# Two mixture-of-experts blocks: wide and narrow expert units alternate, and block 2 fetches tokens in fp32 from x less its mean

## The chip, the cores and the metric

The kernel runs on one core of a Trainium2 chip. The time is that of one execution on the device in microseconds (us), the median of three runs. TensorE is PE in the rows (its weight loads PEld), VectorE is DVE, ScalarE is ACT, GpSimd is POOL, SyncE is SP. All loads of weights are issued by SP on one DMA queue.

## The reference

Two transformer blocks of different make, each of two layers, on 256 tokens of 1024 channels. Each layer is a token mixer and then a mixture of 32 experts. For this text only the experts matter; block 1 has hidden width 512 and an RMS norm ahead, block 2 has hidden width 256 and a layer norm ahead.

```python
def hier_moe(h, ...):                       # block 1; block 2's _hier_moe is alike
    g_sel = argmax(h @ wg + bg)             # one of 4 groups of 8 experts
    top_l, top_i = top_k(e_logits[g_sel], 2)  # two experts of that group
    gates = softmax prob of the group * softmax(top_l)
    ...
    hid = silu(xi @ w1[e]) * (xi @ w3[e])   # for the tokens xi of expert e
    y[tokens of e] += (hid @ w2[e]) * gate
```

All weights are fp32. The routing depends on the data: how many tokens an expert gets is known only when the layer's logits are.

## The kernel before

The program runs four stages of experts, one per layer (block 1's first and second layer, then block 2's), with a mixer ahead of each. An expert stage is one call of `moe`. It works through 11 *units* one after the other. A wide unit has 2 experts with room for 64 tokens each, a narrow unit 4 experts with room for 32, so either fills 128 rows. Per unit PE does this: *fetch* (L878: the selected tokens are gathered by a product of x with a 0/1 matrix `P`, eight slices of 128 channels, then scaled and shifted into `xg`), the first products (L1018: `xg` times w1 and w3, streamed as `w<-A`), and, one unit later, the second products (L932: the hidden values `ht` times w2, streamed as `w<-B`) and the combination (L945). The fetch of the next unit lies between the products of the present one.

The order of units was the same in both blocks: five wide, five narrow, one wide. `PLACES` held (fixed, wide) for each block. The first `fixed` places (4 in block 1, 6 in block 2) are experts by number, whose weights can be asked for in advance. All later places are filled by rank: the class `Ranks` counts the tokens of each late expert, sends those with over 32 to wide places, and gives the order as the tile `kidx`. That comes from a DVE tile `kperm`, a PE product (L724) and a DVE copy (L726). SP reads `kidx` at L753 into registers that address the loads, and can issue no load of a ranked expert before that.

The weight stream goes through a ring of slots of 1 MB: 13 and `EXTRA` more during an expert stage (9 in block 1, 5 in block 2). A load waits at L170 until the last reader of its slot is done. A wide unit in block 1 takes 8 slots of w1 and w3 and 4 of w2, a narrow one twice that; in block 2 half of these. Before `kidx` SP can issue 20 slots in block 1 and 16 in block 2. At the ninth unit after the first (`turn`) stands a branch for experts with over 64 tokens, `overfull` (L767), not taken here; SP waits there until all its loads have landed.

In block 2 the fetch is done with rounded parts: DVE normalises x (L841), ACT rounds it to `xh` (L842), DVE forms the rest `xl` (L851), and the fetch multiplies both by `P` in fp32r, for pairs of units of one kind at a time (256 columns; the first unit and the last narrow and wide ones have 128). In block 1 the fetch is one fp32 product of x itself, and `P` holds the token's norm factor in place of 1. The head of the expert stage (`Head.finish`, L593 to L613) makes the norm's factor and the logits; then the router makes `ras` (chosen experts), `rpos` (the token's place) and `P`.

Of the kernel before, what the change touches and what calls it, by code (L numbers as in the profile page):

```python
# [28 lines left out]
E = 32  # L29
# [22 lines left out]
class Core:  # L52
# [25 lines left out]
    def constants(self, ctx):  # L78
# [31 lines left out]
        self.tok = cp.tile([128, 2, 3], F32, name="tok")  # L110
# [423 lines left out]
class Head:  # L534
# [57 lines left out]
    def finish(self, t):  # L592
# [4 lines left out]
        if self.centred:  # L597
            mv = p.tile([128, 2], F32, name=f"hmv{t}")
            nc.vector.bn_aggr(mv, self.st[:, t])
            nc.vector.tensor_copy(c.tok[:, t, 1:2], mv[:, 0:1])  # L600
            nc.scalar.activation(l[:, 0:1], mv[:, 1:2], AF.Ln, bias=c.col(self.eps))
        else:
            nc.vector.tensor_scalar(l[:, 1:2], self.st[:, t, 0:1], 1.0 / D, self.eps, op0=ALU.mult, op1=ALU.add)
            nc.scalar.activation(l[:, 0:1], self.st[:, t, 1:2], AF.Ln, scale=1.0 / D, bias=l[:, 1:2])
# [6 lines left out]
        else:  # L611
            nc.scalar.activation(c.tok[:, t, 2:3], l[:, 0:1], AF.Exp, scale=0.5)
# [71 lines left out]
class Ranks:  # L684
# [4 lines left out]
    def __init__(self, c, p, ps, as_, fixed, wide):  # L689
# [122 lines left out]
def moe(c, ctx, index, scale, shift, w13, w2, nf, spare, centred, residual, end):  # L812
# [5 lines left out]
    fixed, wide = PLACES[centred]  # L818
# [3 lines left out]
    if centred:  # L822
        groups, k = [units[:1]], 1
        while k < len(units):
            m = 2 if k + 1 < len(units) and units[k + 1][2] == units[k][2] else 1
            groups.append(units[k:k + m])
            k += m
    else:
        groups = [[u] for u in units]
    most = max(map(len, groups)) * 128  # L830
# [6 lines left out]
    if centred:  # L837
# [5 lines left out]
    else:  # L843
        src = (x,)
    pos, as_, rest, chosen = router(c, p, mp, c.L)
    if centred:
        with tc.issue_after(chosen.ins):
            for t in range(2):
                for i in range(2):
                    d = slice(i * 512, i * 512 + 512)  # L850
# [3 lines left out]
    def group(us, first):  # L854

        e0, _, cap = us[0]
        n = sum(u[1] for u in us)
        m = n * cap
        P = p.tile([128, 2, most], F32R if centred else F32, name="P", bufs=2)
        P4 = P[:, :, :m].rearrange("p t (g s) -> p t g s", s=cap)  # L860
        xg = p.tile([128, 8, most], F32, name="xg", tag="xg", bufs=2)

        def select():
            at = pos if e0 < fixed else places["pos"]
            for t in range(2):
                if centred:
                    selected = nc.vector.tensor_tensor(P4[:, t], c.iota[:, None, :cap].to_broadcast([128, n, cap]),
                                                       at[:, t, e0:e0 + n, None].to_broadcast([128, n, cap]),
                                                       ALU.is_equal)
                else:  # L870
                    for i in range(n):
                        selected = nc.vector.tensor_scalar(P4[:, t, i], c.iota[:, :cap], at[:, t, e0 + i:e0 + i + 1],
                                                           c.tok[:, t, 0:1], op0=ALU.is_equal, op1=ALU.mult)
            return selected

        def products(q, k, i, start, stop):
            for t in range(2):
                nc.tensor.matmul(q, src[i][:, t, k * 128:(k + 1) * 128], P[:, t, :m],  # L878
                                 start=start and t == 0, stop=stop and t == 1, skip_group_check=True)

        def modulate(q, k, vector):
            o = xg[:, k, :m]
# [5 lines left out]
        def fetch(k):  # L888
            def f():
                q = mp.tile([128, 512], F32, name="ms")[:, :m]  # L890
                for i in range(len(src)):
                    products(q, k, i, i == 0, i == len(src) - 1)
# [3 lines left out]
        def fetch_all():  # L896
            qs = [yp.tile([128, 512], F32, name="y", tag="y", bufs=4) for _ in range(4)]
            for i in range(len(src)):
                for k in range(8):
                    q = qs[k % 4][:, (k // 4) * m:(k // 4 + 1) * m]  # L900
                    products(q, k, i, i == 0 and k < 4, i == len(src) - 1)
                    if i == len(src) - 1:
                        modulate(q, k, k % 2)
        return P4, xg, [select] + ([fetch_all] if first else [fetch(k) for k in range(8)])

    P, xg, steps = group(groups[0], True)
# [3 lines left out]
    with tc.issue_after(selected.ins):  # L910
        ranks = Ranks(c, p, mp, as_, fixed, wide)
        places["pos"] = ranks.ordered(pos, "kpos")
        w, cnt = rest(ranks.excess)
    wp = w
    if not centred:

        wp = p.tile([128, 2, 32], F32, name="rwp")
        nc.vector.tensor_mul(wp, w, c.tok[:, :, 2:3].to_broadcast([128, 2, 32]))
# [30 lines left out]
    def back(pr, j):  # L949
# [3 lines left out]
        nc.vector.tensor_mul(Pw.rearrange("p t (g s) -> p t g s", s=cap), P[:, :, j:j + ne, :].bitcast(F32),  # L953
# [22 lines left out]
    for g, us in enumerate(groups):  # L976
        if g:
            P, xg = nxt[:2]
        nxt = group(groups[g + 1], False) if g + 1 < len(groups) else (None, None, [])
        share = -(-len(nxt[2]) // len(us))  # L980
        for unit in us:
            e0, ne, cap = unit
            j = e0 - us[0][0]
            n = units.index(unit)
            last = n == len(units) - 1
            todo = [nxt[2].pop(0) for _ in range(min(share, len(nxt[2])))]
            pr = {"n": n, "unit": unit, "h": []}
            who = experts(unit)
            begun = None
            if n == turn - 1:  # L990

                keep = c.hold(extra)
                held = None if centred else c.hold(extra)
                out, gate = residual(mp, keep, c.scratch(), held)
            if n == turn:
                begun = first(who, 0)
                room, hT = [c.scratch(), c.scratch()], c.scratch()
                hT = hT.rearrange("p (a b) -> p a b", b=256)
                count = nc.values_load(cnt[0:1, 0:1], min_val=0, max_val=E * CAP,
                                       skip_runtime_bounds_check_because="counts of tokens")  # L1000
                overfull(c, sp, None if centred else c.tok, scale, shift, out, w, pos, count, nf, *spare, gate, room,
                         hT, ranks)
                c.loaded = None
# [1267 lines left out]
```

## Time and profile before

| | |
|---|---|
| median of three runs | 2426.05 us (2425.70 to 2428.39) |
| the profiled execution | 2428.38 us, span 2426.6 us |
| PE busy | 2149.3 us, 89% of the span |
| DVE, ACT busy | 885.9 us (37%), 751.9 us (31%) |
| DMA queue of the weight loads | 772.85 MB, 79.7% of the 16 engines' span |
| TensorE clock, mean granted | 0.955 |
| expert stages, roughly | 293 to 768, 919 to 1395, 1650 to 1897, 2165 to 2412 us |

Shares are averages over unlike stages; in the expert stages both PE and the DMA engines are near full, and which of them waits changes with the kind of unit.

### The profile page before, as it was taken

What the parts mean: (1) busy time and instruction counts of PE and PEld (TensorE: products, weight loads), DVE (VectorE), ACT (ScalarE), POOL (GpSimd) and SP (SyncE); (2) the same over time, 40 slices, a digit from 0 to 9 for tenths busy, and PEclk for the clock granted to TensorE, in tenths of its full rate; (3) what the DMA queues carried; (4) which work ended last, traced back from release to release, by engine and by line L of the source; (5) the groups of instructions that cost most, each with busy time, mean ns of one, the idle gap of its engine ahead of it and who ended that gap; (6) DMA issues with size and microseconds to landing.
All of it is one profiled execution on the core that took longest, in us unless ns stands there. A gap on an engine that the chain in (4) does not pass through costs nothing. (4 is left out here: it accounts for less than half of the span.)

```text
span 2426.6 us, 32734 instructions
## 1 busy us (share of the span) xinstructions
PE 2149.3 (89%) x12546; PEld 1230.8 (51%) x12546; DVE 885.9 (37%) x1983; ACT 751.9 (31%) x1493; POOL 44.9 (2%) x48
## 2 busy tenths in 40 slices
PE   7999899987678989999767799998998899999977
PEld 4667633322225864333222287994432678974422
DVE  3864511110013762111000354973121647861112
ACT  3642312211004442222111244562211445642212
POOL 0001000000000200000000000000000000000000
PEclk8999999999999998999999899998999989989998
DMA  9977499999999356999999961556999923549997
GB/s 393 403 271 306 174 397 401 417 421 421 386 421 389 119 217 274 400 418 421 421 420 389 421 243 48 197 195 236 377 413 370 381 92 139 191 157 360 409 393 277
DMA packets 119846, 775.13 MB, mean 319 GB/s; under 512 B 14185, under 2 KB 15593, under 8 KB 35450
## 3 DMA queue, kind: packets, MB, share of 16 engines
q1 hardware_dynamic: 119674, 772.85, 79.7%
q8 instruction: 106, 1.74, 0.3%
q14 instruction: 66, 0.54, 0.1%
HBM read 771.75 MB, written 1.05 MB: 318 GB/s over the span
## 5 line engine op out<-in xcount | busy, mean ns | idle before, releaser
L1018 PE MATMUL s<-w,xg 128*32 128x512 f32 (+1 forms) x3072 | 606.9, 617 | 67.9 <-DMA w<-A 59.8
L932 PE MATMUL s<-w,ht 128*32 128x512 f32 (+1 forms) x1536 | 348.4, 617 | 44.8 <-DMA w<-B 43.0
L1018 PEld LDWEIGHTS s<-w,xg 128*32 128x32 f32 (+1 forms) x3072 | 141.8, 121 | 369.2 <-issue 216.5
L396 PE MATMUL pj<-hi,wh 128*128 128x256 f32 x864 | 243.8, 285 | 3.4 <-ACT sg L1800 2.4
L397 PE MATMUL pj<-lo,wh 128*128 128x256 f32 x864 | 243.3, 283 | 0.0
L398 PE MATMUL pj<-hi,wl 128*128 128x256 f32 x864 | 240.4, 284 | 0.0
L935 DVE SCALAR_TENSOR_TENSOR yl<-s,ws,yh 128x512 fp32r<-128x512 f32 x88 | 66.0, 750 | 357.5 <-ACT yh L934 354.5
L932 PEld LDWEIGHTS s<-w,ht 128*32 128x32 f32 (+1 forms) x1536 | 82.6, 122 | 224.5 <-issue 138.5
L391 ACT ACTIVATE wh<-w 128x512 fp32r<-128x512 f32 x248 | 154.4, 631 | 120.0 <-PE pj L397 89.5
L1022 DVE TENSOR_TENSOR hid<-hid,s 128x256 f32<-128x256 f32 x66 | 27.7, 419 | 439.4 <-ACT hid L1021 439.3
L392 DVE TENSOR_TENSOR wl<-w,wh 128x512 fp32r<-128x512 f32 x248 | 167.2, 689 | 50.3 <-ACT wh L391 45.7
L396 PEld LDWEIGHTS pj<-hi,wh 128*128 128x128 f32 x864 | 166.1, 193 | 9.7 <-ACT sg L1800 2.8
L398 PEld LDWEIGHTS pj<-hi,wl 128*128 128x128 f32 x864 | 164.4, 192 | 4.8 <-issue 2.1
L397 PEld LDWEIGHTS pj<-lo,wh 128*128 128x128 f32 x864 | 166.3, 192 | 0.1
L934 ACT ACTIVATE yh<-s,ws 128x512 fp32r<-128x512 f32 x88 | 60.5, 688 | 323.0 <-PE s L932 290.6
L359 DVE TENSOR_TENSOR wl<-w,wh 128x512 fp32r<-128x512 f32 (+2 forms) x164 | 112.6, 695 | 100.1 <-ACT wh L358 83.9
L1021 ACT ACTIVATE hid<-s 128x256 f32<-128x256 f32 x66 | 25.3, 384 | 394.3 <-PE s L1018 394.1
L886 ACT ACTIVATE xg<-ms,mod,gain 128x128 f32<-128x128 f32 x160 | 72.8, 457 | 204.8 <-PE ms L878 202.4
L358 ACT ACTIVATE wh<-w 128x512 fp32r<-128x512 f32 (+2 forms) x164 | 99.6, 614 | 114.5 <-PE pj L344 56.1
L878 PEld LDWEIGHTS ms<-P,x 128*128 128x128 f32 x640 | 85.3, 197 | 66.5 <-issue 35.8
L344 PE MATMUL pj<-wl,hi 128*128 128x512 f32 (+2 forms) x272 | 107.1, 395 | 0.0
L878 PE MATMUL ms<-P,x 128*128 128x128 f32 x640 | 103.7, 294 | 2.0 <-issue 1.6
(638 smaller groups left out, 2731.2 us busy)
## 6 DMA issues: line engine op xcount, KB each, us to landing
w<-A SPq DMA_DIRECT2D x384, 1024.0 KB, 12.1
w<-B SPq DMA_DIRECT2D x128, 1024.0 KB, 17.9
w<-B SPq DMA_DIRECT2D x128, 512.0 KB, 10.2
w<-ada SPq DMA_DIRECT2D x48, 1024.0 KB, 9.8
w<-wi SPq DMA_DIRECT2D x48, 1024.0 KB, 9.4
w<-w SPq DMA_DIRECT2D x26, 1024.0 KB, 15.6
w<-wo SPq DMA_DIRECT2D x16, 1024.0 KB, 5.8
w<-wbr SPq DMA_DIRECT2D x8, 1024.0 KB, 4.8
```

Source lines behind the costliest of these rows:

```text
L344: nc.tensor.matmul(qs[t][:, :n], a, wl[:, :n], start=False, stop=False)
L358: nc.scalar.activation(wh[:, :n], w[:, k], AF.Copy)
L359: nc.vector.tensor_sub(wl[:, :n], w[:, k], wh[:, :n].bitcast(F32))
L391: nc.scalar.activation(wh, w[:, k], AF.Copy)
L392: nc.vector.tensor_sub(wl, w[:, k], wh.bitcast(F32))
L396: nc.tensor.matmul(d, wh[:, e], hi, start=k == 0 and ch % 2 == 0, stop=False, skip_group_check=True)
L397: nc.tensor.matmul(d, wh[:, e], lo, start=False, stop=False, skip_group_check=True)
L398: nc.tensor.matmul(d, wl[:, e], hi, start=False, stop=k == nk - 1, skip_group_check=True)
L878: nc.tensor.matmul(q, src[i][:, t, k * 128:(k + 1) * 128], P[:, t, :m], start=start and t == 0, stop=stop and t == 1, skip_group_check=True)
L886: nc.scalar.activation(o, q, AF.Identity, bias=shift[:, k:k + 1], scale=scale[:, k:k + 1])
L932: nc.tensor.matmul(q[cap * i:cap * i + cap, :], ht[:, o * cap:o * cap + cap], pr["w2"][i][:, half, f * 512:f * 512 + 512], start=f == 0, s ...
L1018: nc.tensor.matmul(q[cap * i:cap * i + cap, :], xg[:, k, e * cap:(e + 1) * cap], ws[m][:, k, 512 * o:512 * o + 512], start=k == 0, stop=k ...
```

## The change

Four parts. `PLACES` now holds the order of units as a string: in block 1 w w n w n w n w n n w, in block 2 w w w n w n w n n n w; the numbers of wide and narrow units stay, and so do the three units at the branch. `Ranks` gets the list `at`, which says which rank stands at which place. In block 2 the normalisation on DVE and the parts `xh` and `xl` go; instead ACT takes the mean from x in place (L612, in the head), `P` holds the norm factor as in block 1, the token weights are multiplied by its inverse, and the fetch is the fp32 product of block 1, unit by unit. `EXTRA` is 9 in both blocks.

```diff
@@ Head.finish
         if self.centred:
             mv = p.tile([128, 2], F32, name=f"hmv{t}")
             nc.vector.bn_aggr(mv, self.st[:, t])
-            nc.vector.tensor_copy(c.tok[:, t, 1:2], mv[:, 0:1])
+            nc.vector.tensor_scalar(c.tok[:, t, 1:2], mv[:, 0:1], -1.0, None, op0=ALU.mult)
...
-        else:
-            nc.scalar.activation(c.tok[:, t, 2:3], l[:, 0:1], AF.Exp, scale=0.5)
+
+            nc.scalar.activation(c.x[:, t], c.x[:, t], AF.Identity, bias=c.tok[:, t, 1:2])
+        nc.scalar.activation(c.tok[:, t, 2:3], l[:, 0:1], AF.Exp, scale=0.5)
@@ Ranks.__init__
-        nc.vector.tensor_copy(row[:, 0:wide - 2], c.places[:, 0:wide - 2])
-        nc.vector.tensor_copy(row[:, wide - 2:E - 2], c.places[:, wide:E])
-        nc.vector.tensor_copy(row[:, E - 2:E], c.places[:, wide - 2:wide])
+        i = 0
+        while i < E:
+            n = 1
+            while i + n < E and at[i + n] == at[i] + n:
+                n += 1
+            nc.vector.tensor_copy(row[:, i:i + n], c.places[:, at[i]:at[i] + n])
+            i += n
@@ moe
-    units = [(n, 2, CAP) for n in range(0, wide - 2, 2)] + [(n, 4, CAP // 2) for n in range(wide - 2, E - 2, 4)]
-    units.append((E - 2, 2, CAP))
...
+    units, at = [], []
+    wide = 2 * form.count("w")
+    nextw, nextn = 0, wide
+    for f in form:
+        n = 2 if f == "w" else 4
+        units.append((len(at), n, 128 // n))
+        if f == "w":
+            at, nextw = at + list(range(nextw, nextw + n)), nextw + n
+        else:
+            at, nextn = at + list(range(nextn, nextn + n)), nextn + n
...
-        src = [p.tile([128, 2, 1024], F32R, name=n) for n in ("xh", "xl")]
-        for t in range(2):
-            nc.vector.tensor_scalar(x[:, t], x[:, t], c.tok[:, t, 1:2], c.tok[:, t, 0:1], op0=ALU.subtract, op1=ALU.mult)
-            nc.scalar.activation(src[0][:, t], x[:, t], AF.Copy)
...
-                    nc.vector.tensor_sub(src[1][:, t, d], x[:, t, d], src[0][:, t, d].bitcast(F32))
...
-        def products(q, k, i, start, stop):
+        def products(q, k, start):
             for t in range(2):
-                nc.tensor.matmul(q, src[i][:, t, k * 128:(k + 1) * 128], P[:, t, :m],
-                                 start=start and t == 0, stop=stop and t == 1, skip_group_check=True)
+                nc.tensor.matmul(q, x[:, t, k * 128:(k + 1) * 128], P[:, t], start=start and t == 0, stop=t == 1,
+                                 skip_group_check=True)
...
-EXTRA = (9, 5)
-PLACES = ((4, 12), (6, 12))
+EXTRA = (9, 9)
+PLACES = ((4, "wwnwnwnwnnw"), (6, "wwwnwnwnnnw"))
```

How it moves instructions shows on PE between the first fetch product of an expert stage and the product that yields `kidx`. This is PE in block 2's first layer before, from behind the first 24 fetch products (rounded parts `xh` and `xl`) on; `s` is the bank of the first unit's first products, `kperm,places` the product that gives `kidx`. The second layer reads the same.

```order
L709 MATMUL ms<-kover,kafter 32x1
L710 MATMUL ms<-kover,lt 32x1
L711 MATMUL ms<-ones,kover 128x1
L878 MATMUL y<-P,xl 128x128 x2
L1018 MATMUL s_12376<-w,xg 64x512 x2
L878 MATMUL y<-P,xl 128x128 x2
L1018 MATMUL s_12376<-w,xg 64x512 x2
L878 MATMUL y<-P,xl 128x128 x2
L1018 MATMUL s_12376<-w,xg 64x512 x2
L878 MATMUL y<-P,xl 128x128 x2
L1018 MATMUL s_12376<-w,xg 64x512 x3
L724 MATMUL ms<-kperm,places 1x32
```

After the change the same place reads thus, behind eight fp32 fetch products of x; each of these is two instructions in a trace.

```order
L714 MATMUL ms<-kover,kafter 32x1
L715 MATMUL ms<-kover,lt 32x1
L716 MATMUL ms<-ones,kover 128x1
L861 MATMUL y<-P,x 128x128 x2
L992 MATMUL s_12386<-w,xg 64x512 x2
L861 MATMUL y<-P,x 128x128 x2
L992 MATMUL s_12386<-w,xg 64x512 x2
L861 MATMUL y<-P,x 128x128 x2
L992 MATMUL s_12386<-w,xg 64x512
L861 MATMUL y<-P,x 128x128 x2
L992 MATMUL s_12386<-w,xg 64x512 x4
L729 MATMUL ms<-kperm,places 1x32
```

The number of first products ahead of `kidx` is nine in both; the fetch products are 16 in place of 32. In block 2's second layer the scheduler now puts only five ahead:

```order
L861 MATMUL y<-P,x 128x128 x8
L714 MATMUL ms<-kover,kafter 32x1
L715 MATMUL ms<-kover,lt 32x1
L716 MATMUL ms<-ones,kover 128x1
L861 MATMUL y<-P,x 128x128 x2
L992 MATMUL s_17185<-w,xg 64x512 x2
L861 MATMUL y<-P,x 128x128 x2
L992 MATMUL s_17185<-w,xg 64x512 x2
L861 MATMUL y<-P,x 128x128 x4
L992 MATMUL s_17185<-w,xg 64x512
L729 MATMUL ms<-kperm,places 1x32
```

There `kidx` has moved ahead of four first products. In block 1 it moves the other way. This is PE in block 1's second layer before, the same place:

```order
L878 MATMUL y<-P,x 128x128 x8
L709 MATMUL ms<-kover,kafter 32x1
L710 MATMUL ms<-kover,lt 32x1
L711 MATMUL ms<-ones,kover 128x1
L878 MATMUL y<-P,x 128x128 x2
L1018 MATMUL s_6750<-w,xg 64x512 x2
L878 MATMUL y<-P,x 128x128 x2
L1018 MATMUL s_6750<-w,xg 64x512 x2
L878 MATMUL y<-P,x 128x128 x4
L1018 MATMUL s_6750<-w,xg 64x512
L724 MATMUL ms<-kperm,places 1x32
```

And now:

```order
L861 MATMUL y<-P,x 128x128 x8
L714 MATMUL ms<-kover,kafter 32x1
L715 MATMUL ms<-kover,lt 32x1
L716 MATMUL ms<-ones,kover 128x1
L861 MATMUL y<-P,x 128x128 x4
L992 MATMUL s_6762<-w,xg 64x512 x4
L861 MATMUL y<-P,x 128x128 x2
L992 MATMUL s_6762<-w,xg 64x512 x2
L861 MATMUL y<-P,x 128x128 x2
L992 MATMUL s_6762<-w,xg 64x512 x3
L729 MATMUL ms<-kperm,places 1x32
```

Nine first products stand ahead of `kidx` where five stood (in the first layer seven where five stood). The other engine on the way to `kidx` is DVE, here in block 2's first layer before, from the choice of experts to the selection matrix:

```order
L645 MATCH_REPLACE rrep<-rt_12220,rel 128x32 x2
L646 TENSOR_SCALAR ras<-rrep 128x64
L851 TENSOR_TENSOR xl<-x,xh 128x512 x4
L651 SCALAR_TENSOR_TENSOR rpos<-ms,ras 128x64
L867 TENSOR_TENSOR P<-iota,rpos 128x128 x2
L694 COPY krow<-places 32x10
L695 COPY krow<-places 32x20
```

And now:

```order
L646 MATCH_REPLACE rrep<-rt_12242,rel 128x32 x2
L647 TENSOR_SCALAR ras<-rrep 128x64
L652 SCALAR_TENSOR_TENSOR rpos<-ms,ras 128x64
L855 TENSOR_SCALAR P<-iota,rpos,tok 128x64 x4
L700 COPY krow<-places 32x6
L700 COPY krow<-places 32x4
L700 COPY krow<-places 32x2
```

The four operations on `xl` ahead of `rpos` are gone, `P` is made by four operations in place of two, and the copies to `krow` (seven now, three before) stand behind it.

## Rows read from the trace of the kernel before

**Rows 1.** Window, block 2's first experts: length; PE, PEld, DVE, ACT, POOL; clock, DMA, GB/s.

```profile
1650.00:1897.00 247.00, 226.03 (x1156) 91.40 (x1156) 50.48 (x124) 52.12 (x100) 0.00 (x0) 0.94 0.90 358
```

**Rows 2.** Windows of block 1: wide units in both layers; narrow units in the first.

```profile
320.00:440.00 120.00, 116.95 (x540) 46.86 (x540) 18.36 (x51) 26.03 (x56) 0.00 (x0) 1.00 0.99 405
950.00:1070.00 120.00, 116.95 (x542) 46.71 (x542) 18.35 (x51) 25.40 (x54) 0.00 (x0) 1.00 0.99 403
450.00:500.00 50.00, 48.04 (x334) 18.68 (x326) 8.34 (x27) 10.83 (x24) 0.00 (x0) 1.00 1.01 421
```

**Rows 3.** SyncE's own waits in 320:440: line, releaser, us in total, times, longest.

```profile
SPq L170 <- PE s L1018: 70.3, 25, 7.0
```

**Rows 4.** Timeline of PE, first fetch product and kidx product: block 1's two layers, block 2's first.

```profile
293.44 3.66 PE L878 MATMUL y<-P,x 128*128 128x128 f32 x16 [0.59 <-DVE P L872]
...
302.94 0.21 PE L724 MATMUL ms<-kperm,places 32*1 32x32 f32 x2
...
919.47 3.75 PE L878 MATMUL y<-P,x 128*128 128x128 f32 x16 [0.68 <-DVE P L872]
...
931.32 0.21 PE L724 MATMUL ms<-kperm,places 32*1 32x32 f32 x2
...
1652.80 3.65 PE L878 MATMUL y<-P,xh 128*128 128x128 f32 x16 [1.59 <-DVE P L867]
...
1668.29 0.21 PE L724 MATMUL ms<-kperm,places 32*1 32x32 f32 x2
```

**Rows 5.** Windows of 10 us, block 1: the stream's first hole in either layer.

```profile
330.00:340.00 10.00, 10.00 (x47) 3.88 (x48) 3.24 (x9) 2.44 (x5) 0.00 (x0) 1.00 0.99 371
960.00:970.00 10.00, 10.00 (x47) 3.70 (x46) 3.24 (x9) 2.06 (x5) 0.00 (x0) 1.00 0.97 356
```

**Rows 6.** Timeline of PE: a fetch slice in block 1, then one in block 2.

```profile
357.30 0.71 PE L878 MATMUL ms<-P,x 128*128 128x128 f32 x4
357.94 2.79 PE L932 MATMUL s<-w,ht 128*64 128x512 f32 x10
...
1695.98 0.48 PE L878 MATMUL ms<-P,xh 128*128 128x256 f32 x2
1696.30 0.40 PE L878 MATMUL ms<-P,xl 128*128 128x256 f32 x2
1696.63 5.36 PE L1018 MATMUL s<-w,xg 128*64 128x512 f32 x22
```

**Rows 7.** Windows of block 2, wide units: undisturbed, then the holes of both layers.

```profile
1680.00:1690.00 10.00, 10.00 (x50) 4.39 (x48) 0.00 (x0) 3.38 (x6) 0.00 (x0) 1.00 1.00 394
...
1700.00:1730.00 30.00, 29.85 (x132) 12.36 (x129) 5.85 (x13) 7.32 (x14) 0.00 (x0) 1.00 0.94 360
2220.00:2250.00 30.00, 29.85 (x136) 11.95 (x134) 6.60 (x14) 7.72 (x15) 0.00 (x0) 1.00 0.92 352
```

**Rows 8.** Windows around the rise of the clock: block 1's first layer, block 2's first.

```profile
296.80:303.00 6.20, 6.20 (x36) 3.25 (x35) 2.99 (x13) 1.37 (x3) 0.00 (x0) 1.00 0.00 0
...
1652.80:1665.60 12.80, 12.80 (x48) 8.35 (x48) 5.43 (x29) 3.50 (x7) 0.00 (x0) 0.50 0.00 0
```

**Rows 9.** Timeline of block 2's head, first layer: rounded parts, place matmul, rpos.

```profile
1645.56 2.16 ACT L842 ACTIVATE xh<-x 128x1024 fp32r<-128x1024 f32 x2
...
1649.70 2.49 DVE L851 TENSOR_TENSOR xl<-x,xh 128x512 fp32r<-128x512 f32 x4
...
1650.32 0.58 PE L649 MATMUL ms<-ras,ones 128*128 128x32 f32 x2
...
1652.11 0.22 DVE L651 SCALAR_TENSOR_TENSOR rpos<-ms,ras 128x64 f32<-128x64 f32 x1
```

**Rows 10.** Window around the branch in block 2's first layer.

```profile
1835.00:1860.00 25.00, 15.99 (x77) 3.26 (x79) 0.68 (x2) 0.38 (x1) 0.00 (x0) 0.93 0.82 309
```

**Rows 11.** PE's groups in 1676:1900 (narrow second products), and one run in the timeline.

```profile
L932 PE MATMUL s<-w,ht 128*32 128x512 f32 x160 | 34.0, 614 | 3.5 <-DMA w<-B 3.4
...
1886.67 1.92 PE L932 MATMUL s<-w,ht 128*32 128x512 f32 x14
```

More of the change, by code (lines that the diff above doesn't have):

```diff
@@ L817, in moe @@
     nc, tc, x = c.nc, c.tc, c.x
-    fixed, wide = PLACES[centred]
-    units = [(n, 2, CAP) for n in range(0, wide - 2, 2)] + [(n, 4, CAP // 2) for n in range(wide - 2, E - 2, 4)]
-    units.append((E - 2, 2, CAP))
[L822 to L830, printed above, removed]
+    fixed, form = PLACES[centred]
+    units, at = [], []
[8 more added lines that the diff above has]
+            at, nextn = at + list(range(nextn, nextn + n)), nextn + n
     steps_of = 1 if centred else 2
@@ L836, in moe, with group @@
     extra = c.more(ctx, EXTRA[centred], "ring2", *XO[index])
-    if centred:
-        src = [p.tile([128, 2, 1024], F32R, name=n) for n in ("xh", "xl")]
-        for t in range(2):
-            nc.vector.tensor_scalar(x[:, t], x[:, t], c.tok[:, t, 1:2], c.tok[:, t, 0:1], op0=ALU.subtract, op1=ALU.mult)
-            nc.scalar.activation(src[0][:, t], x[:, t], AF.Copy)
-    else:
-        src = (x,)
-    pos, as_, rest, chosen = router(c, p, mp, c.L)
[L846 to L850, printed above, removed]
-                    nc.vector.tensor_sub(src[1][:, t, d], x[:, t, d], src[0][:, t, d].bitcast(F32))
-    places = {"pos": pos}
[L854 to L861, printed above, removed]
+    pos, as_, rest, chosen = router(c, p, mp, c.L)
+    places = {"pos": pos}
+    def group(unit, first):
+        e0, n, cap = unit
+        P = p.tile([128, 2, 128], F32, name="P", bufs=2)
+        P4 = P.rearrange("p t (g s) -> p t g s", s=cap)
+        xg = p.tile([128, 8, 128], F32, name="xg", tag="xg", bufs=2)
         def select():
@@ L889, in f @@
             def f():
-                q = mp.tile([128, 512], F32, name="ms")[:, :m]
-                for i in range(len(src)):
-                    products(q, k, i, i == 0, i == len(src) - 1)
+                q = mp.tile([128, 512], F32, name="ms")[:, :128]
+                products(q, k, True)
                 modulate(q, k, False)
@@ L897, in fetch_all @@
             qs = [yp.tile([128, 512], F32, name="y", tag="y", bufs=4) for _ in range(4)]
[L898 to L903, printed above, removed]
+            for k in range(8):
+                q = qs[k % 4][:, (k // 4) * 128:(k // 4 + 1) * 128]
+                products(q, k, k < 4)
+                modulate(q, k, k % 2)
         return P4, xg, [select] + ([fetch_all] if first else [fetch(k) for k in range(8)])
-    P, xg, steps = group(groups[0], True)
+    P, xg, steps = group(units[0], True)
     selected = steps[0]()
@@ new lines, in moe @@
+        nxt = group(units[n + 1], False) if n + 1 < len(units) else (None, None, [])
+        e0, ne, cap = unit
+        last = n == len(units) - 1
+        todo = nxt[2]
+        pr = {"n": n, "unit": unit, "h": []}
+        who = experts(unit)
+        begun = None
+        if n == turn - 1:
+            keep = c.hold(extra)
+            held = None if centred else c.hold(extra)
+            out, gate = residual(mp, keep, c.scratch(), held)
+        if n == turn:
+            begun = first(who, 0)
+            room, hT = [c.scratch(), c.scratch()], c.scratch()
+            hT = hT.rearrange("p (a b) -> p a b", b=256)
+            count = nc.values_load(cnt[0:1, 0:1], min_val=0, max_val=E * CAP,
+                                   skip_runtime_bounds_check_because="counts of tokens")
+            overfull(c, sp, c.tok, scale, shift, out, w, pos, count, nf, *spare, gate, room,
+                     hT, ranks)
+            c.loaded = None
+            who, prev["who"] = experts(unit), experts(prev["unit"])
@@ L1048, in moe @@
+        if centred:
+            for f in todo[half:]:
+                f()
+        pr["who"] = who
+        if last and not centred:
+            for t in range(2):
+                nc.vector.tensor_add(c.x[:, t], c.x[:, t], out[:, t])
+        back(pr)
+        prev = pr
     outer(prev, prev["who"])
```

140 lines of the change are left out of this document (51 added, 89 removed).

## The prediction

> **What bounds the kernel now.** I read the expert stages first, because the change touches little else. In the expert stage of block 2's first layer TensorE is busy 226 of 247 us and the DMA engines 90% of the time [rows 1] (the second layer's window reads 226.07 and 0.88). So two engines share the bound, and the question is which of them waits where. Windows cut by unit kind answer it. While the wide units run in block 1 (320 to 440, and 950 to 1070) PE is busy 117 of 120 us and the stream moves 405 and 403 GB/s; when narrow units follow it moves 421 [rows 2]. The reader is to see the inversion: with wide units PE is full and the stream has holes, with narrow units the stream is full and PE has holes. SyncE's own waits name the holes: in 320:440 the load line waited 70.3 us for slots that L1018's matmuls still held [rows 3]. Before the stream starts, both engines stand behind the ranking of the late experts: SP can issue nothing for a ranked expert until `kidx` exists, and `kidx` comes out of the PE row L724 [rows 4].
>
> **What the new order gives in block 1.** A hole in the stream is lost bandwidth. (421-405)/421 x 120 = 4.6 us in the first layer, (421-403)/421 x 120 = 5.1 in the second [rows 2]. When a narrow unit stands between wide ones, PE has slack in it to catch up, and the slots that it frees let the stream run on through the next wide unit. The first two units stay wide, so the first hole stays: (421-371)/421 x 10 = 1.2 us and (421-356)/421 x 10 = 1.5 [rows 5]. Against this `kidx` comes later: two more L1018 matmuls stand ahead of L724 in the first layer, four more in the second (order rows). Each is two instructions; 22 of them took 5.36 us [rows 6], so 0.49 a matmul, 1.0 and 2.0 us. A stream that starts later meets the first hole shorter, so the larger of hole and delay counts: 4.6-1.2 = 3.4 and 5.1-2.0 = 3.1. Together **6.5 us**. Bounds: nothing regained and both delays paid, 3 us lost; all holes closed, no delay, 9.7 gained.
>
> **What it gives in block 2.** The same holes: 360 GB/s over 30 us in the first layer, 352 in the second, where the undisturbed stream ran 394 [rows 7]. Against 394 that is 2.6 and 3.2 us, against 421 4.3 and 4.9. I take 3.0 and 3.6, near the first, as half-size loads run here too. The four slots more are part of this price: the stream is now stopped by a held slot, and 22 slots let it lead by four loads more.
>
> `kidx` comes earlier. From the first fetch product to L724 block 2 takes 1668.29-1652.80 = 15.5 us, block 1 9.5 and 11.85 [rows 4] (block 2's second layer repeats its first, 15.4). The number of fetch instructions is not what differs: 32 one-instruction rounded products are replaced by 16 fp32 products of two instructions, and 16 instructions took 3.65 us of the one and 3.66 of the other at the low clock [rows 4]. What differs is the clock. The granted clock stood at 0.50 (1.2 GHz) for all 12.8 us after block 2's first product, with PE busy throughout; in block 1 it was 1.00 (2.4 GHz) from 296.8, 3.4 us after the first fp32 product [rows 8]. In the second layer block 1 stayed low longer, which its 11.85 contains. So I price the new sequence by block 1's two rows. First layer: still nine L1018 ahead, four more than block 1's five, so 9.5+2.0 = 11.5 to 11.85+2.0 = 13.8, a gain of 1.7 to 4.0; I take the middle, 2.85. Second layer: five, a gain of 3.6 to 5.9; middle 4.75.
>
> The TensorE page of the Trainium skill (TensorE: Matmul & The Clock Gate, "What's actually happening") says that the low clock is the default and that activity releases it; it makes no difference between the kinds of product. The trace disagrees to the extent that the rounded products kept PE busy 12.80 of 12.80 us and released nothing; by the page's rule the new products need not do better, and the two gains would fall to the third rival's.
>
> The head before the fetch I count at nothing. Removed: the four L851 (2.49 us) between `ras` and `rpos`. Added: the two Identity activations on ACT, now ahead of the second `hT` and the second Exp; L842's two of that size took 2.16 [rows 9], so 1.1 us each, of which the second falls on the path to the logits; and `P` is again four operations, about half a microsecond more. The matmuls that `rpos` needs ended at 1650.90 and `rpos` began at 1652.11 [rows 9], so 1.2 gained against some 1.6 lost; bounds 1 either way. The longer row of `krow` copies lies under PE's fetch.
>
> Sums: first layer 2.85+3.0 = 5.85, second 4.75+3.6 = 8.35, **14.2 us** if the stream sets the end.
>
> **What it costs.** The fetch doubles on PE. In block 1 one slice of one unit takes 357.94-357.30 = 0.64 us; in block 2 a slice for two units takes 1696.63-1695.98 = 0.65 [rows 6]. Ten units of eight slices: up to 51 us, against 4 pairs x 8 x 0.65 = 20.8 and two single units of 2.6 to 5.1 each, 26 to 31. Added: **20 to 25 us a layer**; I take 20, since slices that follow one another cost under 0.64. Cover: PE has 21 idle us in the stage [rows 1]. Of these 9 lie at the turn (1835:1860, busy 16 of 25 [rows 10]), where SP drains its loads before the overfull branch; unit kinds there are unchanged (n n w), and I leave them. But more idle is hidden in busy rows: L932's narrow instructions are counted 34.0 us for 160, 0.21 each, where an undisturbed run of them takes 1.92 for 14, 0.137 [rows 11]; up to 12 us are waits for w2 that vanish when loads are ahead. The earlier clock adds about 3. So 21-9+12+3 = 27 of cover for 20 at best, 15 at worst. It just fits: I charge 1 us a layer, between 0 and 5. If the cover is gone, every further microsecond falls on the end.
>
> **Sum.** 6.5+14.2-2 = 18.7 us. The profiled run took 2428.4 (span 2426.6, 1.8 around it), so 2409.7. It stands 2.3 above the median of the three, so I forecast **2407 us** as the median. All favourable ends (6.7 in block 1 with its first holes, 4.0+4.3 and 5.9+4.9 in block 2) give 26 and about 2400.
>
> **Rivals.**
> (1) *PE becomes block 2's bound.* Half of the hidden waits come back, the fetch adds 22; 4 us a layer more are lost: 2407+8 = 2415. For it: PE full from 1700 to 1730 [rows 7] and thin cover. Against: the narrow units in which PE waits for w now.
> (2) *The same, wholly, and the kernel is slower.* If L932's narrow instructions are slow by themselves and the fetch costs 25, PE's stage is 226+25+9-3 = 257 against 247: 10 lost a layer, 20-6.5 = 13.5, 2439. It decides from an addition of 21 us a layer with nothing given back. Against: the 0.137 row.
> (3) *The clock rises no sooner.* Then the first layer gains nothing from `kidx`, the second the time of four matmuls, 2 to 2.5: 5.3 less, 2412. For it: the same clock in both layers of block 2; against: block 1's rows.
> (4) *The alternation does nothing*: the holes are of another kind than held slots, or move. 6.5 and 6.6 less, with `kidx` in block 2 still gained: 2420, and 2423 if both of block 1's delays are paid in full. Against: SP's row [rows 3].
>
> The DMA page of the Trainium skill (DMA: Bandwidth & Descriptors, "Where 436 GB/s comes from") speaks for (4): it puts loads from HBM at about 358 GB/s for a core. At that a wide unit's 12.6 MB would take 35 us, an estimate from its figure, and no order of units would matter in block 1. The 421 GB/s of rows 2 decide against it.
>
> **How the numbers follow.** Chances: forecast 0.57, (1) 0.15, (2) 0.07, (3) 0.12, (4) 0.09. A measurement of this kernel tells 0.2% (4.9 us) from no change. Faster by more: forecast, (1), (3), most of (4), less its tails, 0.85; within 0.2% 0.08; slower 0.07. The range takes in the favourable end and all but (2) and part of (4): 2398 to 2419. The forecast's own range is 2400 to 2412.
>
> **What would show it.** In the profile after: block 1's 320 to 440 at 415 GB/s or more; `kidx` about 1 and 2 us later in block 1, about 3 and 5 earlier after the first fetch product in block 2; a granted clock of 1.00 well before 12.8 us there; block 2's PE busier by about 20 us less hidden waits and idle outside the turn under 10; its stages 5 and 7 us shorter. I am wrong if block 2's stream shows more holes than now with PE full (1, 2), if the clock row repeats (3), or if block 1's stages keep their length (4).

## The result, and the profile after

The changed kernel takes 2402.53 us (median of four runs, 2400.36 to 2405.39) against 2427.22 us for the kernel before, a ratio of 0.9899 with a 95% interval of 0.9882 to 0.9916. On another chip, beside the last experiments, it took 2401.05 (ratio 0.9884, 0.9867 to 0.9900). The forecast was 2407, the range 2398 to 2419.

The profiled execution has a span of 2398.6 us, 28.0 less than before. I cut both traces at the first fetch product and the end of the last combination product of each expert stage. Block 1's stages went from 460.1 and 462.4 us to 458.0 and 459.6, block 2's from 244.3 and 244.7 to 234.2 and 233.4; all that lies between and around them gave 1.7. So 4.9 of the 28 us are block 1's and 21.4 block 2's. The second profile of the same kernel (changed_again) is 4 us longer and gives 3.4 and 18.1.

Windows of the kernel after, columns as in [rows 1]; they answer to [rows 2, 1, 7] in this order, and the last one, around the branch in block 2's first layer, to [rows 10]:

```profile
320.00:440.00 120.00, 116.78 (x646) 44.96 (x646) 17.48 (x50) 25.82 (x57) 0.00 (x0) 1.00 1.01 418
950.00:1070.00 120.00, 116.68 (x652) 45.03 (x652) 18.20 (x51) 25.16 (x54) 0.00 (x0) 1.00 1.01 421
1646.00:1881.00 235.00, 229.20 (x1276) 99.45 (x1276) 58.63 (x174) 64.27 (x132) 0.00 (x0) 0.99 0.94 379
...
1690.00:1720.00 30.00, 29.84 (x176) 12.29 (x174) 7.81 (x23) 8.74 (x19) 0.00 (x0) 1.00 1.02 417
...
1825.00:1850.00 25.00, 23.03 (x152) 10.29 (x152) 3.01 (x6) 6.67 (x15) 0.00 (x0) 1.00 0.82 301
```

The reader is to see that PE is as busy as before where wide units run, while the stream beside it is now full: 418 and 421 GB/s for 405 and 403, and 417 in block 2 for 360. In block 2's stage PE is busy 229 of 235 us, where it was 226 of 247: the stage became shorter by PE's idle time, not by PE's work.

SyncE's own waits in 320:440 of the kernel after (line, releaser, us, times, longest), to set beside [rows 3]:

```profile
SPq L170 <- PE s L992: 31.4, 12, 7.1
SPq L170 <- DMA w<-A: 30.4, 17, 2.0
```

The waits for slots that a first product still holds fell from 70.3 to 31.4 us; waits behind the stream itself came in their place. The timeline of PE, first fetch product and product of `kidx` in all four stages after, beside [rows 4]:

```profile
293.28 3.78 PE L861 MATMUL y<-P,x 128*128 128x128 f32 x16 [0.58 <-DVE P L855]
...
303.70 0.21 PE L729 MATMUL ms<-kperm,places 32*1 32x32 f32 x2
916.59 3.75 PE L861 MATMUL y<-P,x 128*128 128x128 f32 x16 [0.68 <-DVE P L855]
...
930.44 0.21 PE L729 MATMUL ms<-kperm,places 32*1 32x32 f32 x2
1646.41 3.48 PE L861 MATMUL y<-P,x 128*128 128x128 f32 x16 [0.59 <-DVE P L855]
...
1657.79 0.21 PE L729 MATMUL ms<-kperm,places 32*1 32x32 f32 x2
2151.54 3.50 PE L861 MATMUL y<-P,x 128*128 128x128 f32 x16 [0.59 <-DVE P L855]
...
2160.88 0.21 PE L729 MATMUL ms<-kperm,places 32*1 32x32 f32 x2
```

`kidx` comes 10.4 and 13.9 us behind the first fetch product in block 1 (before 9.5 and 11.85) and 11.4 and 9.3 in block 2 (before 15.5 and 15.4). The clock in block 2's first layer, the window of the first eight fetch products and the next, answers to [rows 8]:

```profile
1646.40:1649.80 3.40, 3.39 (x16) 3.29 (x16) 3.27 (x25) 2.21 (x5) 0.00 (x0) 0.55 0.03 10
1649.80:1655.00 5.20, 5.20 (x29) 2.63 (x28) 2.69 (x13) 1.27 (x3) 0.00 (x0) 1.00 0.00 0
```

It is at 1.00 after 3.4 us, where it took 12.8. The second layer rises as early here; changed_again will show that this was luck.

### The profile page after: what moved, and what is told of

Read it like the earlier page. It is cut to its first block, busy times and chain, and to the rows that moved or that the text cites. A ratio compares the mean times of both kernels' runs of the same rounds, so it can differ in the third digit from the quotient of the medians.

```text
span 2398.6 us, 33422 instructions
## 1 busy us (share of the span) xinstructions
PE 2166.9 (90%) x12802; PEld 1248.4 (52%) x12802; DVE 899.5 (38%) x2095; ACT 775.4 (32%) x1561; POOL 44.9 (2%) x48
## 5 line engine op out<-in xcount | busy, mean ns | idle before, releaser
L992 PE MATMUL s<-w,xg 128*32 128x512 f32 (+1 forms) x3072 | 580.7, 612 | 37.7 <-DMA w<-A 36.4
L910 PE MATMUL s<-w,ht 128*32 128x512 f32 (+1 forms) x1536 | 341.5, 618 | 38.2 <-DMA w<-B 36.5
L992 PEld LDWEIGHTS s<-w,xg 128*32 128x32 f32 (+1 forms) x3072 | 133.0, 120 | 302.2 <-issue 197.1
L861 PEld LDWEIGHTS ms<-P,x 128*128 128x128 f32 x1280 | 169.5, 194 | 140.5 <-ACT xg L869 74.5
L861 PE MATMUL ms<-P,x 128*128 128x128 f32 x1280 | 207.8, 292 | 2.1 <-issue 1.1
L855 DVE TENSOR_SCALAR P<-iota,kpos,tok 128x32 f32<-128x32 f32 (+1 forms) x216 | 49.3, 299 | 306.9 <-PE ms L861 306.9
```

The costliest lines, as they stand in the source:

```text
L861: nc.tensor.matmul(q, x[:, t, k * 128:(k + 1) * 128], P[:, t], start=start and t == 0, stop=t == 1, skip_group_check=True)
L910: nc.tensor.matmul(q[cap * i:cap * i + cap, :], ht[:, o * cap:o * cap + cap], pr["w2"][i][:, half, f * 512:f * 512 + 512], start=f == 0, s ...
L992: nc.tensor.matmul(q[cap * i:cap * i + cap, :], xg[:, k, e * cap:(e + 1) * cap], ws[m][:, k, 512 * o:512 * o + 512], start=k == 0, stop=k ...
```

## The experiments

The theory: block 2's wide units held the stream's slots, and narrow units between them let PE catch up (*order*); the fp32 fetch brings the clock and `kidx` forward (*clock*). The chief rival: the four slots more bridged the wide units and the order did little (*slots*). A second: PE was far from the bound, or is now alone the bound.

All runs in one table. Ratios are to the kernel before on the same chip, with the 95% interval; kidx is the time behind the first fetch product in block 2's two layers, and the four lengths are those of the expert stages, each from the run's profiled execution.

| run | median us | ratio | kidx, block 2 | stages, us |
|---|---|---|---|---|
| before | 2427.22 | 1 | 15.5, 15.4 | 460.1, 462.4, 244.3, 244.7 |
| changed | 2402.53 | 0.9899 (0.9882 to 0.9916) | 11.4, 9.3 | 458.0, 459.6, 234.2, 233.4 |
| changed_again | 2401.05 | 0.9884 (0.9867 to 0.9900) | 11.3, 12.2 | 459.5, 459.7, 234.6, 236.2 |
| slots5 | 2420.72 | 0.9963 (0.9949 to 0.9978) | 11.4, 14.3 | 459.4, 459.8, 242.4, 245.8 |
| order2 | 2417.75 | 0.9957 (0.9944 to 0.9969) | 11.4, 12.7 | 459.8, 458.8, 242.3, 242.7 |
| order12 | 2424.36 | 0.9986 (0.9977 to 0.9994) | 11.4, 12.8 | 462.8, 462.4, 240.4, 241.2 |
| alternate_only | 2417.02 | 0.9959 (0.9946 to 0.9972) | 15.4, 16.9 | 457.6, 459.6, 241.7, 240.8 |
| first_fp32 | 2423.38 | 0.9978 (0.9967 to 0.9990) | 13.3, 11.7 | 462.3, 463.0, 243.9, 239.5 |
| fetch_twice | 2476.38 | 1.0196 (1.0181 to 1.0210) | 14.3, 9.3 | 457.4, 459.9, 275.0, 272.7 |
| fetch_half | 2399.90 | 0.9883 (0.9867 to 0.9900) | 11.3, 12.1 | 457.0, 459.8, 232.6, 233.7 |
| kidx_first | 2401.30 | 0.9886 (0.9871 to 0.9900) | 8.2, 8.2 | 457.7, 457.7, 235.2, 236.3 |
| kidx_first_mean_late | 2400.47 | 0.9890 (0.9874 to 0.9907) | 5.8, 8.2 | 457.7, 458.0, 231.9, 235.6 |
| keep_busy | 2399.03 | 0.9876 (0.9859 to 0.9892) | 11.9, 13.2 | 456.8, 456.6, 234.5, 235.2 |
| keep_busy_kidx | 2394.81 | 0.9863 (0.9847 to 0.9880) | 6.7, 5.3 | 455.1, 456.9, 233.8, 233.8 |

**slots5**, the changed kernel with block 2's slots as before.

```diff
-EXTRA = (9, 9)
+EXTRA = (9, 5)
```

> The changed kernel with block 2's stream slots back at 18 (five extra instead of nine); all else as changed. Order theory: the narrow units between wide ones give PE the slack, 18 slots are enough, and the time stays within 2 us of the changed kernel's 2402.5, say 2403 to 2405. Slots theory: the fp32 fetch keeps PE so full that slots come free late, and four slots of lead were what kept the stream running; block 2's stream then shows holes of 4 to 6 us a layer and the time is 2411 to 2414. In the second layer nine first products stand ahead of kidx instead of five, which alone is 2 us.

The slots theory's size, and more: 2420.7. Windows of block 2's first layer:

```profile
1660.00:1690.00 30.00, 29.40 (x146) 13.37 (x142) 6.36 (x22) 7.94 (x17) 0.00 (x0) 1.00 0.97 390
1690.00:1720.00 30.00, 29.95 (x176) 12.36 (x174) 6.73 (x22) 8.77 (x18) 0.00 (x0) 1.00 0.80 295
1720.00:1760.00 40.00, 39.83 (x234) 16.97 (x234) 9.10 (x25) 11.99 (x25) 0.00 (x0) 1.00 1.02 416
```

The hole lies where the first three wide units end, (421-295)/421 x 30 = 9.0 us; once a narrow unit has passed, the stream is full. So the order can't mend the first three units, and the slots do: in the changed kernel the window 1690:1720 moves 417. The time is 6 us above what the slots theory had; in the second layer `kidx` comes later as well, 14.3 us behind.

**order2**, the changed kernel with block 2's old order.

```diff
-PLACES = ((4, "wwnwnwnwnnw"), (6, "wwwnwnwnnnw"))
+PLACES = ((4, "wwnwnwnwnnw"), (6, "wwwwwnnnnnw"))
```

> The changed kernel with block 2's units in the old order (five wide, five narrow, one wide); block 1 alternates, fp32 fetch and 22 slots stay. Order theory: PE is over-full through five wide units with the dearer fetch, the stream stops for slots around the fourth unit, and block 2 loses 5 to 8 us a layer: 2412 to 2418. Slots theory: 22 slots bridge the wide units, and the time stays at 2403 to 2405.

2417.8: the order theory's size. The hole has moved to the fourth and fifth wide unit:

```profile
1690.00:1720.00 30.00, 29.87 (x142) 12.65 (x142) 7.80 (x23) 8.71 (x18) 0.00 (x0) 1.00 0.95 366
1720.00:1760.00 40.00, 39.72 (x222) 16.81 (x218) 9.12 (x28) 11.61 (x24) 0.00 (x0) 1.00 0.87 328
```

(421-328)/421 x 40 = 8.8 us. Slots postpone the hole, they don't close it. slots5 and order2 each lose most of the change's gain, so each needs the other.

**order12**, the old order in both blocks.

```diff
-PLACES = ((4, "wwnwnwnwnnw"), (6, "wwwnwnwnnnw"))
+PLACES = ((4, "wwwwwnnnnnw"), (6, "wwwwwnnnnnw"))
```

> The changed kernel with the old order in both blocks. Against order2 only block 1 changes: its stages took 2.1 and 2.8 us less in the changed kernel's profile. If that is the alternation, this run is 4 to 6 us above order2; if the two stages became shorter for another reason, it equals order2.

6.6 us above order2 in the medians, a little more than expected, and, in block 1's two stages of the profiled executions, 3.0 and 3.6. Block 1's gain is the alternation. Block 2's stages, alike in both programs, differ by 1.9 and 1.5 us the other way: that is how far a stage's length moves from one profile to another.

**alternate_only**, the kernel before with the new order alone (`units`, `at` and `Ranks` as in the change).

```diff
-PLACES = ((4, 12), (6, 12))
+PLACES = ((4, "wwnwnwnwnnw"), (6, "wwwnwnwnnnw"))
```

> The kernel before with the new order of units in both blocks and nothing else: rounded parts, pairs of like units where two stand together, 18 slots in block 2. Order theory: block 1 gains its 5 us, block 2 closes its holes at a cheap fetch, 4 to 7 us a layer, kidx stays 15.5 us behind the first fetch product: 2427 less 13 to 19, 2408 to 2414. If the fp32 fetch and the slots were what filled block 2's stream, only block 1's 5 us come, 2422.

2417.0, between the two expectations, so neither was right. Block 1 has its gain; in block 2 the stream has a small hole left behind the third wide unit and is full then:

```profile
1690.00:1720.00 30.00, 30.00 (x168) 11.70 (x166) 5.76 (x13) 6.40 (x13) 0.00 (x0) 1.00 0.98 381
1720.00:1760.00 40.00, 39.93 (x250) 18.49 (x248) 7.18 (x16) 13.14 (x28) 0.00 (x0) 1.00 1.02 417
```

The parts don't add: the order alone gives 0.41%, fetch and slots without the order 0.14% (order12), together 0.55%; the whole change gives 1.0 to 1.2%. The dearer fetch without its slots (slots5) gives nothing that alternate_only doesn't have. The four slots with the rounded parts were not run.

**first_fp32**, the kernel before, the first unit's fetch of block 2 in fp32.

```diff
+            if centred:
+                for k in range(8):
+                    q = qs[k % 4][:, (k // 4) * m:(k // 4 + 1) * m]
+                    for t in range(2):
+                        nc.tensor.matmul(q, x[:, t, k * 128:(k + 1) * 128], P[:, t, :m].bitcast(F32),
+                                         start=k < 4 and t == 0, stop=t == 1, skip_group_check=True)
+                    modulate(q, k, k % 2)
+                return
```

> The kernel before, but the first unit of block 2's stages is fetched by 16 fp32 products of the normalised x instead of 32 products of its rounded parts; the later units keep the rounded parts, order and slots are as before. Clock theory: the fp32 products bring TensorE's clock up sooner, and kidx comes 10 to 13 us behind the first fetch product (seven first products ahead in the first layer, six in the second) where it was 15.5 and 15.4; the median falls by 4 to 9 us, 2419 to 2424. Rival: the clock rises as late as before, kidx comes 14 us or more behind, and the median falls by 3 us or less. The rounded parts are still formed ahead of the places in the head, so what is gained there is not in this run.

`kidx` came 13.3 and 11.7 us behind, the second as the clock theory had it, the first just above:

```profile
1655.83 3.79 PE L903 MATMUL y<-P,x 128*128 128x128 f32 x16 [1.50 <-DVE P L867]
...
1669.12 0.21 PE L724 MATMUL ms<-kperm,places 32*1 32x32 f32 x2
...
2169.04 3.78 PE L903 MATMUL y<-P,x 128*128 128x128 f32 x16 [1.50 <-DVE P L867]
...
2180.78 0.21 PE L724 MATMUL ms<-kperm,places 32*1 32x32 f32 x2
```

The clock stood at 0.50 for 9.3 and 8.1 us behind the first fetch product, where it had been 12.8 and 12.7:

```profile
1655.83:1665.10 9.27, 9.27 (x36) 6.72 (x38) 5.34 (x29) 3.05 (x6) 0.00 (x0) 0.50 0.00 0
1665.10:1668.00 2.90, 2.90 (x16) 1.24 (x12) 0.00 (x0) 0.46 (x1) 0.00 (x0) 1.00 0.00 0
```

The median fell by 4.6 us, at the low end; two and three first products fewer stand ahead of `kidx` here, each 0.5 to 1.0 us long by the clock (22 instructions in 5.36 us, [rows 6], four in 1.98 at 0.50), so 1 to 2 of the 2.2 us and 1.5 to 3 of the 3.7 are not the clock.

**fetch_twice** and **fetch_half**: block 2's fetch products from the second unit on issued twice, and half of them left out (each even slice used for the odd one as well, which changes the result).

```diff
-                products(q, k, True)
+                for _ in range(2 if centred else 1):
+                    products(q, k, True)
```

```diff
+                if centred and k % 2:
+                    return
                 q = mp.tile([128, 512], F32, name="ms")[:, :128]
                 products(q, k, True)
                 modulate(q, k, False)
+                if centred:
+                    modulate(q, k + 1, False)
```

> The changed kernel with every fetch product of block 2's second to eleventh unit issued twice; the result is the same. It adds once more the time that the fp32 fetch takes on PE, 42 us a layer, where the change added 15. If PE had cover left for the change's 15 and little more, nearly all of it shows: 30 to 42 us a layer, 2462 to 2486. If PE were far from the bound, under 20 us a layer, below 2443.

> The changed kernel with half of block 2's fetch left out: from the second unit on only the even slices are computed, and each is used for the odd one too, so the output is not the reference's. About 21 us of PE a layer are gone. If the changed kernel's block 2 is held by PE and the stream together, the stream holds the end at once and 1 to 4 us a layer come off: 2394 to 2401. If PE alone holds it, 10 or more a layer: below 2385.

Twice the fetch lengthens block 2's stages by 40.8 and 39.2 us, as much as the added products take: counted from the start of each PE instruction to the start of the next, idle time left out, the fetch of units two to eleven holds PE for 82.6 us in the first layer here, for 44.1 in the changed kernel and for 21.4 in the halved one (27.6 in the kernel before). Half of it shortens them, against changed_again, by 2.1 and 2.5 (against the first profile by 1.6 and, in the second layer, not at all); the median by 1.2, inside the intervals. The window of the halved one's first layer:

```profile
1646.00:1879.00 233.00, 211.08 (x1116) 80.98 (x1116) 58.56 (x173) 59.11 (x132) 0.00 (x0) 0.99 0.93 380
```

PE has 22 us idle again and the end hardly moved. So in the changed kernel PE and the stream end together: what is added to PE shows at once, what is taken from it doesn't.

**changed_again** is the changed kernel once more.

> The changed kernel once more, beside the next three on the same chip: 2400 to 2406, ratio near 0.990. Its profile shows whether the clock's rise in the expert stages' heads moves from one execution to the next.

It agrees in time. The first 10 us after the first fetch product in block 2's two layers:

```profile
1647.45:1657.45 10.00, 10.00 (x52) 6.65 (x54) 6.41 (x39) 3.40 (x7) 0.00 (x0) 0.86 0.00 1
2152.75:2162.75 10.00, 10.00 (x38) 6.72 (x38) 6.04 (x37) 3.05 (x6) 0.00 (x0) 0.52 0.07 28
```

The first rises early again (0.86 of full speed on the mean), the second late (0.52), and the second's stage is 2.8 us longer than in the first profile: the same program, another moment of the clock.

**kidx_first** and **kidx_first_mean_late**. In the changed kernel `kperm` was ready 3.6 to 6.7 us before PE came to the product that gives `kidx`, which stood behind first products. The first orders these behind it; the second also lets ACT take the mean from x only after both Exp operations.

```diff
-        nc.tensor.matmul(q[0:1, 0:E], num, self.perm, start=True, stop=True)
+        self.asked = nc.tensor.matmul(q[0:1, 0:E], num, self.perm, start=True, stop=True)
...
+                    if n == 0:
+                        tc.add_manual_dep(mm.ins, ranks.asked.ins.name, ...)
```

```diff
-            nc.scalar.activation(c.x[:, t], c.x[:, t], AF.Identity, bias=c.tok[:, t, 1:2])
-        nc.scalar.activation(c.tok[:, t, 2:3], l[:, 0:1], AF.Exp, scale=0.5)
+        late = nc.scalar.activation(c.tok[:, t, 2:3], l[:, 0:1], AF.Exp, scale=0.5)
...
+        if self.centred and t == 1:
+            for u in range(2):
+                less = nc.scalar.activation(c.x[:, u], c.x[:, u], AF.Identity, bias=c.tok[:, u, 1:2])
+                c.tc.add_manual_dep(less.ins, late.ins.name, ...)
```

> The changed kernel with the first unit's first products ordered behind the product that yields kidx, in all four expert stages; nothing else. kperm was ready 4.5, 6.9, 5.8 and 3.8 us before that product ran, so kidx can come 3 to 6 us earlier in each stage. If the stream sets the end, most of this comes back at the end: 10 to 18 us, 2385 to 2393. If PE sets the end in block 2, or the first hole grows by as much as the stream starts earlier, 5 us or less: 2397 or above.

> As kidx_first, and in block 2's head ACT takes the mean from x only behind both Exp operations, so that the logits don't wait for it. The two Identity operations took 1.14 us each ahead of hT and Exp, so the first fetch product should come about 1 us earlier in each layer of block 2: 1 to 3 us less than kidx_first. If x then comes too late for the fetch, nothing or a loss.

The second of the two outcomes came, and it is the most telling run. In kidx_first `kidx` came 8.2 us behind the fetch in all four stages, 1.1 to 5.6 earlier than in the changed kernel, and the time is the same (0.9886). Two things took it. In block 1 and in block 2's first layer the holes grew, and in block 2 PE had next to no idle time left. Windows of kidx_first, first two with holes, then block 2's two stages whole:

```profile
330.00:340.00 10.00, 10.00 (x46) 3.65 (x44) 3.24 (x9) 2.45 (x5) 0.00 (x0) 1.00 0.75 272
1700.00:1720.00 20.00, 20.00 (x120) 8.61 (x123) 4.32 (x12) 6.13 (x13) 0.00 (x0) 1.00 0.92 337
...
1647.68:1882.90 235.22, 230.82 (x1276) 101.89 (x1276) 57.36 (x172) 64.15 (x132) 0.00 (x0) 0.97 0.94 376
2152.85:2389.12 236.27, 231.91 (x1276) 101.99 (x1276) 57.28 (x172) 64.28 (x132) 0.00 (x0) 0.97 0.91 366
```

The first hole in block 1 has 3.5 us, against 1.2 in [rows 5] and 0.7 in the changed kernel (390 GB/s in the same window), and block 2 has one of 4.0 where the changed kernel moves 418. PE was not ahead, so the slots were not. In block 2's stages PE is idle 4.4 us each, and was idle 5.0 and 4.7 in the changed kernel: its own work nearly fills them. This profile has the late rise of the clock in all four stages, so its lengths are not quite comparable with the first profile's; the medians don't rest on it. Letting the mean come late brought the first fetch product 0.7 us forward and gave 0.8 us in the median, inside the spread: the 1 to 3 us expected did not show.

**keep_busy** and **keep_busy_kidx**: ten products of constants on PE, whose result nobody reads, between the last logits product and the router's; alone, and with kidx_first_mean_late.

```diff
+    q = ps.tile([128, 512], F32, name="ms")
+    for i in range(BUSY):
+        mm = nc.tensor.matmul(q[:, 0:128], c.id, c.ones, start=True, stop=True)
+        c.tc.add_manual_dep(mm.ins, c.last.ins.name, ...)
```

> The changed kernel with ten products of constants, whose result nobody reads, on PE behind each expert stage's last logits product, where PE waits for the router and its clock falls. Clock theory: the clock is still at 1.00 when the fetch begins, the first unit's products take half, and each stage of block 2 becomes 1.5 to 4.5 us shorter, block 1's 0 to 2: 2390 to 2399. Rival: the clock falls all the same or the products delay the router's, then no gain or a loss, 2402 and above.

> keep_busy together with kidx_first_mean_late: the stream starts earlier and PE is ahead as well, so that the first hole should not grow as it did in kidx_first. If both theories hold, 2386 to 2396 and lower than keep_busy; if the earlier stream only makes a larger hole, equal to keep_busy.

keep_busy gave 2 us in the median, inside the intervals: in both of its block 2 stages the clock fell as the fetch began or just ahead of it. keep_busy_kidx gave 2394.8 (2393.1 to 2397.1); all its runs lie below all of changed_again's (2399.1 to 2404.4) on that chip, though the ratios' intervals overlap. The median lies where it was expected if both theories hold. Its second layer of block 2, from the head to `kidx` (windows, then the timeline):

```profile
2140.00:2144.40 4.40, 2.97 (x27) 2.66 (x27) 3.35 (x21) 0.72 (x1) 0.00 (x0) 1.00 0.94 342
2144.40:2149.70 5.30, 4.69 (x39) 4.29 (x40) 5.01 (x36) 3.33 (x7) 0.00 (x0) 1.00 0.35 140
...
2195.00:2215.00 20.00, 19.97 (x128) 8.08 (x124) 4.74 (x15) 6.33 (x13) 0.00 (x0) 1.00 0.92 363
```

```profile
2144.42 2.62 PE L873 MATMUL y<-P,x 128*128 128x128 f32 x20 [0.77 <-DVE P L867]
...
2149.68 0.21 PE L741 MATMUL ms<-kperm,places 32*1 32x32 f32 x2 [0.59 <-DVE kperm L739]
```

Here the clock never fell, ten fetch products took 2.6 us and `kidx` came 5.3 behind. At 2195 the hole is back, 2.8 us: the stream is again ahead of PE. It is the fastest version run. But its profile has the gain in block 1, whose stages are 2.9 and 2.7 us shorter than in the changed kernel's first profile; block 2's, 233.8 us each, are as long as there (234.2 and 233.4). PE's work in them is some 2.5 us less than there, and its idle time has grown by 2.1 and 2.8:

```profile
1638.69:1872.49 233.80, 226.69 (x1276) 98.62 (x1276) 57.25 (x172) 64.08 (x132) 0.00 (x0) 0.99 0.95 384
2144.42:2378.26 233.84, 226.36 (x1276) 97.49 (x1276) 56.70 (x172) 64.11 (x132) 0.00 (x0) 0.99 0.93 372
```

## Why the prediction was right

The median lies 4.5 us under the forecast and inside its range. Block 1 came out a little under its sum, block 2, with 18.1 to 21.4 us for 14.2 less the charge of 2, well over it; the range held because it reached to the favourable ends.

**Block 1.** Forecast 6.5 us, measured 4.9 in the profiled pair, 3.4 by changed_again's profile and 6.6 by order12 against order2. The two delays of `kidx` were 0.9 and 2.0 us (forecast 1.0 and 2.0), in changed_again, where the first layer's clock rose late, 2.7 and 1.8; the windows 418 and 421 GB/s (forecast 415 or more). The mechanism held, and the size within what a stage's length moves. In the sum of favourable ends block 1 without its first holes is 9.7-1.2-1.5 = 7.0, not 6.7; the end stays about 2400.

**kidx in block 2.** Forecast 2.85 and 4.75 us earlier, measured 4.1 and 6.1, in changed_again 4.2 and 3.2. The clock did rise sooner, and the pricing by block 1's two rows held. The 6.1 is luck, though: in ten profiles with the fp32 fetch (all but keep_busy and keep_busy_kidx) the clock rose early in the second layer in two, in the first layer in seven, so 3.2 is the likelier gain. In the profiles with the rounded parts (before and alternate_only) the clock stayed low for 12 us or more after the first fetch product in all four of block 2's stages; with the fp32 fetch it rose after about 3 or after 8 to 10 us in each of those ten. That was rival (3), and it fell. But the reason that I gave for its worth was half of it. I took an earlier `kidx` to be an earlier end. kidx_first moved `kidx` alone and gained nothing. The early clock also takes work off PE: between the two profiles of the changed kernel block 2's second layer differs by 2.9 us in `kidx` and by 2.8 in length. That an earlier `kidx` pays once the clock is early too is shown by the medians of keep_busy and keep_busy_kidx alone; for block 2 it is not shown, as keep_busy_kidx's stages there did not get shorter; a single stage of kidx_first_mean_late, 231.9 us with `kidx` at 5.8 and an early clock, points that way.

**The stream in block 2** is the mis-sized term. I took 394 GB/s as the undisturbed rate and holes of 3.0 and 3.6 us. Behind `kidx` the stages became 6.0 and 5.1 us shorter. The stream now runs at 417 in 1690:1720, with half-size loads as before, so 394, read from ten us, was too low a reference. SyncE's waits that reach into those ten us (kernel before, 1680:1690) were already for slots that PE held, though the DMA share read 1.00:

```profile
SPq L170 <- PE s L1018: 5.9, 1, 5.9
SPq L170 <- PE s L932: 5.5, 1, 5.5
```

With the 421 that block 1 showed, [rows 7] would have given 4.3 and 4.9.

**The cost on PE.** Forecast 20 to 25 us of fetch a layer, with a charge of 1 for what is not covered. By the count given with fetch_twice the fetch of ten units holds PE for 44 us, where I had put up to 51, and held it for 28; the change adds 16.5. The cover was larger than I thought, too: the 9 us of idle at the branch, which I left out of it, went to 2 (the window 1825:1850), where PE, as I read it, had loads ahead of it to work on while SP drained; with half the fetch gone the same 25 us have 7.7 us of idle again. But "it just fits" was right in the end: fetch_twice finds no cover left. The second products, from which I hoped up to 12 us, gave 6 by the same count (59.6 to 53.5, narrow and wide), and the narrow first products, which I had not counted on, another 5 (46.0 to 40.8): the sum was nearly right, its source only by half. In all, PE's busy time in the first layer's stage rose by 4.3 us (224.9 to 229.2). The busy row of the narrow second products, beside [rows 11], shows 2.6 us of their 6:

```profile
L910 PE MATMUL s<-w,ht 128*32 128x512 f32 x160 | 31.4, 600 | 1.6 <-DMA w<-B 1.5
```

So rival (1) was nearer than its 0.15 said: PE has 5 us of idle left in each stage. A fetch cheaper than its price and the idle time at the branch kept it off; that is the arithmetic, no run tests it.

**The head.** Counted at nothing within 1 us: from the last addition to x to the first fetch product it was 10.0 us and is 9.4.

**The four slots** I called part of the same price. They are a condition of it: without them the change is worth 0.37% in place of 1.0 to 1.2%. The kernel with the rounded parts has no room for nine extra slots; removing them makes it, and by slots5 and alternate_only that, more than the products, is what the fp32 fetch is good for.

## What to carry to other kernels

Where two engines bound a stage in turn, mix the kinds of work that load one and the other, and look in windows cut by kind, not at the stage's mean, for which one waits. Buffer slots move a hole to later, order closes it; each gave well under half of the whole here when tried without the other (0.37 and 0.43% of 1.0 to 1.2). An earlier start of a stream gave nothing here while its consumer was full, so try the start alone before pricing it.

## What the runs showed of the hardware

In the heads of these stages PE's clock falls from 1.00 to 0.50 while PE waits for the router, and the moment of its rise moves between executions of one program: block 2's second layer kept the low clock for 3.1 us after the first fetch product in one profile of the changed kernel and for 9.6 in the other, with `kidx` 9.3 and 12.2 us behind and the stage 233.4 and 236.2 us long. With ten products of constants in the head it was at 1.00 when the fetch began, and until `kidx`, in three of keep_busy_kidx's four stages; in block 2's first layer it fell 0.4 us into the fetch. What decides it stays open.
